# Second convolved tile back in row 6, the first chunks' gate products on VectorE, key-value products later in the recurrence: a two-layer hybrid decoder on one core

## The chip, the cores and the metric

The kernel runs on one core of a Trainium2 chip. Its engines are TensorE (PE in the profile; PEld is its weight load), VectorE (DVE), ScalarE (ACT), GpSimd (POOL) and SyncE (SP), which here only issues DMA transfers. Each engine works through its own queue of instructions in order. The metric is the device time of one execution in microseconds, as the median of several runs. A profile of one execution gives the span from its first to its last instruction.

## What is computed

A decoder of two layers on 1024 tokens of width 1024. Layer 0 mixes tokens with a gated linear recurrence of 8 heads, layer 1 with sliding-window attention; each layer ends with a gated FFN with a causal convolution of width 3. Each sub-layer is followed by a layer norm. Cut to what the change touches:

```python
def hgrn2_chunkwise(q, k, v, log_f):
    # S_t = diag(f_t) S_{t-1} + k_t v_t^T ; o_t = S_t^T q_t, chunk by chunk
    def step(state, inp):
        q_, k_, v_, b_ = inp
        o_inter = jnp.einsum('bhtk,bhkv->bhtv', q_ * jnp.exp(b_), state)
        ...
        o = o_inter + jnp.einsum('bhts,bhsv->bhtv', scores, v_)
        k_dec = k_ * jnp.exp(b_last[:, :, None, :] - b_)
        state = jnp.exp(b_last)[..., None] * state + jnp.einsum('bhsk,bhsv->bhkv', k_dec, v_)
        return state, o

def conv_ffn(h, w_in, conv_w, conv_b, w_out):
    u = h @ w_in
    u = lax.conv_general_dilated(u, conv_w[:, None, :], window_strides=(1,), padding=[(CONV_WIDTH - 1, 0)], ...) + conv_b
    a, b = jnp.split(u, 2, axis=-1)
    return (jax.nn.silu(a) * b) @ w_out
```

The FFN is 2816 wide (w_in is 1024 x 5632), all in float32.

## The kernel before

Every large product is made from a high and a low part of each operand: ScalarE casts a tile to its high part (L249 for weights), VectorE subtracts to get the low part (L197), and TensorE adds three matmuls, high x high, high x low, low x high (`mm3`, L222 to L224). Most products are also cut by a Strassen-like scheme: seven products of half-sized blocks in the place of eight, which need sums of blocks of the weights and of the moving operand, and combinations of the results.

**The order of the work.** In the recurrence the order on all engines is the program's own. A small planner (`Order`) counts TensorE's time in `od.t` while the program is written out. Each piece of a head's work is a generator; a `yield 2.6` says that the next piece is to be emitted once 2.6 us more of TensorE's work have been emitted. In the FFNs only TensorE's order is that of the program; the queues of the other engines, SP's with its DMA issues among them, are ordered by the framework's scheduler from priorities (the program's order) and readiness.

**The recurrence** (`recur`). While the input projections of the next head run in 14 products (`product`, with `evacuate` taking results off the accumulators), the chain of the current head is threaded between them. At its end TensorE turns the decayed keys (8 transposes), ScalarE copies them to `kd` (L1189), the generator pauses at L1190, and TensorE multiplies keys with values (`psax<-VG,kd`, L228 through `mm32`). VectorE then carries the state through the chunks (L1203, L1205), and after another pause TensorE makes the outputs (L1214 to L1217). The chains of the heads follow one another. `VG` holds values and gates of a head and is written by the evacuations of later projections (L1385, L1389).

**The FFN's up-projection** (`Up`). The 2816 columns of each half are made in 22 chunks (`fc`) of 128 for the SiLU half and 128 for the gate half; each chunk has seven products in the order 1, 2, 6, 7, 4, 5, 3 (chunks 0 and 1 are interleaved). A product is 12 matmuls.

- Weights: `weight_load` brings a chunk's two raw pairs of blocks to `rx` buffers (L471), and casts the first. `weight_sums` makes the sums of blocks on VectorE (L480 to L483) and splits them. The raw buffers take turns: `rx[0]`, `rx[1]`, `rx[2]`, and from chunk 2 on also row 7 of `Y`, so that the second pair of chunks 3, 5, 7 and so on goes to row 7, and their first to `rx[2]`.
- Results: `collect` combines the seven results in `Y` rows 0 to 3 (L506 to L520). After product 4 the SiLU half is complete, after product 3 the gate half; each is then convolved: ScalarE writes bias plus the last tap (L526), VectorE adds two shifted taps (L528). The SiLU half is convolved in row 4 or 5 of `Y` (by turns) and passed through SiLU (L531). The gate half is convolved in row 6, in chunk 1 in row 7. Their product (L533) goes back to row 4 or 5, on GpSimd in chunks 0 and 1, on VectorE in the others, and is stored to DRAM (`gd`, L534).
- After chunks 2, 6, 10 and 14 GpSimd's queue adds up blocks of the down-projection's weights by DMA (`bsd`, L549, L551).

Before the up-projection, row 7 of `Y` holds the eighth token block, which is normed, stored and turned (L433 to L445).

Of the kernel before, what the change touches and what calls it, by code (L numbers as in the profile page):

```python
# [14 lines left out]
ALU = mybir.AluOpType  # L15
# [7 lines left out]
NH = 8  # L23
# [111 lines left out]
def trunk(ctx: ExitStack, tc: tile.TileContext, a: dict, out: bass.AP):  # L135
    nc = tc.nc
# [19 lines left out]
    Y = Rows(cp)  # L156
# [239 lines left out]
    tt = nc.vector.tensor_tensor  # L396
# [6 lines left out]
    class Up:  # L403
# [98 lines left out]
        def collect(self, p, fc, ps):  # L502
            l, C = self.l, Y[:, 2 * (fc % 2):2 * (fc % 2) + 2, :]
            C11, C21, C12, C22 = C[:, 0, :512], C[:, 0, 512:], C[:, 1, :512], C[:, 1, 512:]
            if p == 1:
                nc.scalar.copy(C11, ps)  # L506
                nc.scalar.copy(C12, ps)
            elif p == 2:
                tt(C11, C11, ps, op=add)
            elif p == 6:  # L510
                tt(C12, C12, ps, op=add)
            elif p == 7:
                tt(C22, C12, ps, op=add)
            elif p == 4:
                tt(C21, C22, ps, op=add)  # L515
            elif p == 5:
                both = C[:, 1, :].rearrange("p (h n) -> p h n", h=2)
                tt(both, both, ps.unsqueeze(1).to_broadcast([P, 2, 512]), op=add)
            elif p == 3:
                tt(C12, C12, ps, op=add)  # L520
            if p in (4, 3):
                part = 0 if p == 4 else 1
                ci = fc + part * NF
                u, ca = C[:, part, :], Y[:, 4 + fc % 2, :]
                c = Y[:, 7 if fc == 1 else 6, :] if part else ca
                nc.scalar.activation(c, u, AF.Identity, bias=cwt[:, l, 3, ci:ci + 1], scale=cwt[:, l, 2, ci:ci + 1])  # L526
                for sh in (1, 2):
                    nc.vector.scalar_tensor_tensor(c[:, sh:], u[:, :S - sh], cwt[:, l, 2 - sh, ci:ci + 1],  # L528
                                                   c[:, sh:], op0=ALU.mult, op1=ALU.add)
                if part == 0:  # L530
                    nc.scalar.activation(c, c, AF.Silu)  # L531
                else:
                    (nc.gpsimd if fc < 2 else nc.vector).tensor_tensor(ca, ca, c, op=ALU.mult)  # L533
                    nc.sync.dma_start(gd[:, fc, :], ca)  # L534
                    if fc in (2, 6, 10, 14):
                        k = 3 * (fc // 4)
                        self.sums_of_weights(k, min(k + 3, NF // 2), ca[:1, :16])
# [186 lines left out]
    with tc.tile_pool(name="t", bufs=1, reuse_waits="tile") as raws, hgrn_pool as hp:  # L724
# [320 lines left out]
        def recur(h, qs, fg, kp):  # L1045
# [141 lines left out]
            put()  # L1187
            kd = hp.tile([P, S], F32, name="kd")
            nc.scalar.copy(kd, ps)  # L1189
            yield 2.6 if h < NH - 2 else 2.0  # L1190
            while values_in[0] < h:
                yield 0.2
            V = VG[h][:, 0, :].rearrange("p (c d) -> p c d", c=NB)
# [281 lines left out]
        with tc.manual_schedule(engines={EN.PE, EN.SP, EN.Activation, EN.DVE, EN.Pool}):  # L1475
# [11 lines left out]
            def all_heads():  # L1487
                h = -1
                while h < NH - 1:
                    while not ready:  # L1490
                        yield 0.2
                    h, args = ready.pop(0)
                    yield from recur(h, *args)
# [8 lines left out]
            for n, (m, p) in enumerate(line):  # L1502
# [4 lines left out]
                h, g = pairs[m]  # L1507
# [413 lines left out]
```

## Time and profile before

| | us |
|---|---|
| median of 3 runs | 2131.01 |
| lowest, highest run | 2129.49, 2133.35 |
| the profiled execution | 2129.32 |
| its span, first to last instruction | 2127.5 |

The mean granted clock of TensorE over the span is 0.993 of full speed. Layer 0's recurrence takes about the first 460 us, its output projection and FFN run to about 1230, attention to about 1420, and layer 1's FFN to the end.

How to read the rows: a row of a timeline has the start and the duration in us, the engine, the line of the kernel, the operation, the tile written `<-` the tiles read, shapes and a count; in brackets stands how long the engine was idle before it and what ended that. A row of merged instructions gives the time from the first one's start to the last one's end. A row `A <- B: total, times, longest` of the list of waits says how long A waited for B. The name `Y` is that of the whole group of rows, so that rows 4, 6 and 7 have the same name in the profile.

### The profile page before, as it was taken

What the parts mean: (1) busy time and instruction counts of PE and PEld (TensorE: products, weight loads), DVE (VectorE), ACT (ScalarE), POOL (GpSimd) and SP (SyncE); (2) the same over time, 40 slices, a digit from 0 to 9 for tenths busy, and PEclk for the clock granted to TensorE, in tenths of its full rate; (3) what the DMA queues carried; (4) which work ended last, traced back from release to release, by engine and by line L of the source; (5) the groups of instructions that cost most, each with busy time, mean ns of one, the idle gap of its engine ahead of it and who ended that gap; (6) DMA issues with size and microseconds to landing.
All of it is one profiled execution on the core that took longest, in us unless ns stands there. A gap on an engine that the chain in (4) does not pass through costs nothing.

```text
span 2127.5 us, 31578 instructions
## 1 busy us (share of the span) xinstructions
PE 2091.0 (98%) x12303; PEld 1742.4 (82%) x12303; DVE 1777.9 (84%) x2420; ACT 970.5 (46%) x1586; POOL 189.1 (9%) x214
## 2 busy tenths in 40 slices
PE   9999999999989999999999999999989999999998
PEld 8778888787878888888888888888868888888886
DVE  6777777768989999987977679979989999878986
ACT  6556555643534444444433367733444444444430
POOL 1000000001010000000001123312100000000002
PEclk9999999999999999999999999999999999999999
DMA  4111111333256775538755511052275776449662
GB/s 153 41 51 51 51 51 51 118 119 117 80 146 161 183 178 150 142 109 303 248 187 164 143 36 46 18 174 89 70 177 149 178 183 152 121 146 323 228 211 97
DMA packets 239824, 286.82 MB, mean 135 GB/s; under 512 B 30217, under 2 KB 160441, under 8 KB 239417
## 3 DMA queue, kind: packets, MB, share of 16 engines
q1 hardware_dynamic: 223360, 238.26, 34.6%
q0 software_dynamic: 15456, 46.16, 10.9%
q8 instruction: 97, 1.59, 0.3%
q14 instruction: 55, 0.44, 0.1%
q10 hardware_dynamic: 856, 0.37, 0.1%
HBM read 241.72 MB, written 89.15 MB: 156 GB/s over the span
## 4 chain that ended last, share of the span: by engine, by line
PE 68%; DVE 3%; DMA 0%; issue 0%; ACT 0%; POOL 0%; SPq 0%; DVEq 0%; POOLq 0%; ACTq 0%
PE psmm L224 13%; PE psmm L222 12%; PE psmm L223 12%; PE psax L222 9%; PE psax L224 9%; PE psax L223 9%; PE psmm L228 1%; PE psax L1695 1%; PE psmm L232 1%; DVE Y L528 1%; DVE HL L197 0%; PE psax L232 0%; DMA rx<-in_ffn_w_in_dram 0%; DMA Y<-in_ffn_w_in_dram 0%; DVE TX L197 0%
## 5 line engine op out<-in xcount | busy, mean ns | idle before, releaser
L222 PE MATMUL psmm<-T,HL 128*128 128x512 f32 x816 | 322.4, 395 | 0.5 <-DVE VG L758 0.4
L223 PE MATMUL psmm<-T,HL 128*128 128x512 f32 x816 | 318.3, 390 | 0.9 <-DVE T L197 0.9
L224 PE MATMUL psmm<-T,HL 128*128 128x512 f32 x816 | 318.5, 390 | 0.2 <-DVE HL L197 0.2
L528 DVE SCALAR_TENSOR_TENSOR Y<-Y,cwt,Y 128x1023 f32<-128x1023 f32 (+1 forms) x176 | 226.7, 1290 | 47.3 <-ACT Y L526 45.8
L249 ACT CAST HL<-rx 128x1024 fp32r<-128x1024 f32 (+1 forms) x151 | 151.0, 1006 | 175.4 <-DMA rx<-in_ffn_w_in_dram 44.7
L197 DVE TENSOR_TENSOR HL<-rx,HL 128x1024 fp32r<-128x1024 f32 (+1 forms) x151 | 177.1, 1179 | 25.2 <-ACT HL L249 25.0
L224 PEld LDWEIGHTS psmm<-T,HL 128*128 128x128 f32 x816 | 153.3, 188 | 32.7 <-DVE HL L197 0.6
L222 PEld LDWEIGHTS psmm<-T,HL 128*128 128x128 f32 x816 | 153.4, 188 | 31.9 <-DVE VG L758 0.7
L223 PEld LDWEIGHTS psmm<-T,HL 128*128 128x128 f32 x816 | 153.5, 188 | 31.6 <-DVE T L197 1.3
L222 PE MATMUL psax<-T,HL 128*128 128x512 f32 x392 | 153.4, 391 | 0.0
L224 PE MATMUL psax<-T,HL 128*128 128x512 f32 x392 | 152.7, 390 | 0.0
L223 PE MATMUL psax<-T,HL 128*128 128x512 f32 x392 | 152.7, 390 | 0.0
L526 ACT ACTIVATE Y<-Y,cwt 128x1024 f32<-128x1024 f32 x88 | 108.8, 1237 | 91.4 <-DVE Y L515 91.4
L197 DVE TENSOR_TENSOR HL<-raw,HL 128x512 fp32r<-128x512 f32 (+1 forms) x121 | 92.3, 790 | 38.0 <-ACT HL L1303 27.0
L271 POOL TENSOR_TENSOR rs<-rs,nhalf 128x1 f32<-128x1 f32 x32 | 45.0, 1406 | 740.9 <-DVE rs L270 740.9
L249 ACT CAST HT<-rx 128x1024 fp32r<-128x1024 f32 (+1 forms) x37 | 35.5, 959 | 125.2 <-DVE rx L482 48.4
L222 PE MATMUL psmm<-HL 128*128 128x512 f32 x220 | 86.5, 393 | 0.0
L223 PEld LDWEIGHTS psax<-T,HL 128*128 128x128 f32 x392 | 74.0, 189 | 15.3
L222 PEld LDWEIGHTS psax<-T,HL 128*128 128x128 f32 x392 | 73.9, 189 | 15.1
L224 PEld LDWEIGHTS psax<-T,HL 128*128 128x128 f32 x392 | 73.6, 188 | 15.3
L224 PE MATMUL psmm<-HL 128*128 128x512 f32 x220 | 85.8, 390 | 0.0
L223 PE MATMUL psmm<-HL 128*128 128x512 f32 x220 | 85.8, 390 | 0.0
(404 smaller groups left out, 5209.9 us busy)
## 6 DMA issues: line engine op xcount, KB each, us to landing
rx<-in_ffn_w_in_dram SPq DMA_DIRECT2D x136, 256.0 KB
rx<-gd SPq DMA_DIRECT2D x118, 256.0 KB
bsd<-in_ffn_w_out_dram POOLq DMA_DIRECT2D x36, 768.0 KB, 8.2
gd<-Y SPq DMA_DIRECT2D x44, 512.0 KB
raw<-in_hgrn_w_in_dram SPq DMA_DIRECT2D x30, 512.0 KB
rx<-in_ffn_w_out_dram SPq DMA_DIRECT2D x54, 256.0 KB
R<-bsd SPq DMA_DIRECT2D x44, 256.0 KB
Y<-in_ffn_w_in_dram SPq DMA_DIRECT2D x40, 256.0 KB
```

The source lines that it names most:

```text
L197: make = lambda e: e.tensor_tensor(lo, src, hi.bitcast(F32), op=ALU.subtract)
L222: nc.tensor.matmul(ps, st(0), mv(0), start=start, stop=False, skip_group_check=onto)
L223: nc.tensor.matmul(ps, st(0), mv(1), start=False, stop=False, skip_group_check=onto)
L224: nc.tensor.matmul(ps, st(1), mv(0), start=False, stop=stop, skip_group_check=onto)
L228: nc.tensor.matmul(ps, lhsT, rhs, start=start, stop=stop, **kw)
L232: nc.tensor.transpose(ps, src, ident)
L249: nc.scalar.copy(hi, src)
L271: nc.gpsimd.tensor_tensor(rs, rs, nhalf, op=ALU.pow)
L526: nc.scalar.activation(c, u, AF.Identity, bias=cwt[:, l, 3, ci:ci + 1], scale=cwt[:, l, 2, ci:ci + 1])
L528: nc.vector.scalar_tensor_tensor(c[:, sh:], u[:, :S - sh], cwt[:, l, 2 - sh, ci:ci + 1], c[:, sh:], op0=ALU.mult, op1=ALU.add)
L1695: nc.tensor.matmul(self.pv[:, e, jj, lo:], self.q[bp // 2][es, e, qs], Kl[es, pp, ks] if low else Kh[:, pp, e, ks], start=not low and jj = ...
```

## The change

It does three things:

1. The convolved gate half (`c`) lies in row 6 of `Y` in every chunk. Before, chunk 1 used row 7.
2. The gate products of chunks 0 and 1 are made by VectorE, as those of the other chunks already were, two in each layer.
3. The pause between the copy of `kd` and the products of keys with values is 5.0 in heads 0 and 1 and 3.4 in heads 2 to 5; it was 2.6 in heads 0 to 5. Heads 6 and 7 keep 2.0.

```diff
@@ -522,7 +522,7 @@
                 u, ca = C[:, part, :], Y[:, 4 + fc % 2, :]
-                c = Y[:, 7 if fc == 1 else 6, :] if part else ca
+                c = Y[:, 6, :] if part else ca
                 nc.scalar.activation(c, u, AF.Identity, bias=cwt[:, l, 3, ci:ci + 1], scale=cwt[:, l, 2, ci:ci + 1])
@@ -530,7 +530,7 @@
                 else:
-                    (nc.gpsimd if fc < 2 else nc.vector).tensor_tensor(ca, ca, c, op=ALU.mult)
+                    tt(ca, ca, c, op=ALU.mult)
                     nc.sync.dma_start(gd[:, fc, :], ca)
@@ -1187,7 +1187,7 @@
             nc.scalar.copy(kd, ps)
-            yield 2.6 if h < NH - 2 else 2.0
+            yield 5.0 if h < 2 else 3.4 if h < NH - 2 else 2.0
             while values_in[0] < h:
```

`tt` is `nc.vector.tensor_tensor`; `NH` is 8.

## The prediction

> **What bounds the kernel now.** I read the page's busy shares first, then the list of what TensorE waited for, then windows of 40 us, and last the timelines around the waits. The page:
>
> ```profile
> span 2127.5 us, 31578 instructions
> ...
> PE 2091.0 (98%) x12303; PEld 1742.4 (82%) x12303; DVE 1777.9 (84%) x2420; ACT 970.5 (46%) x1586; POOL 189.1 (9%) x214
> ```
>
> TensorE (PE) is idle for 36.5 of 2127.5 us. No matmul is added or removed by the change, so it can win only what TensorE loses: idle time, and matmuls run at a lower clock. Who makes it wait (total, times, longest):
>
> ```profile
> PE psmm L222 <- ACT HL L249: 10.1, 2, 5.3
> PE psax L228 <- ACT kd L1189: 6.0, 3, 2.8
> PE psmm L224 <- DVE HL L197: 2.5, 3, 1.8
> PE psmm L222 <- ACT VG L1385: 0.6, 1, 0.6
> PE psmm L222 <- ACT VG L1389: 0.6, 1, 0.6
> ```
>
> The first and third rows lie in the up-projections of the two FFNs, the second in the recurrence: the two places that the change touches. The windows price the first place (columns: window, length, then busy us and instructions of PE, PEld, DVE, ACT and POOL, granted clock, DMA):
>
> ```profile
> 600.00:640.00 40.00, 34.66 (x140) 27.68 (x139) 32.27 (x39) 17.15 (x20) 3.86 (x5) 0.91 0.71 175
> 640.00:680.00 40.00, 40.00 (x178) 33.15 (x177) 38.37 (x46) 16.66 (x19) 2.43 (x3) 1.00 0.67 169
> 1520.00:1560.00 40.00, 32.91 (x132) 26.31 (x131) 35.71 (x39) 17.46 (x20) 7.80 (x4) 0.87 0.34 108
> ```
>
> An undisturbed 40 us hold 178 matmuls, 0.225 us each. The window of layer 0 holds 140, so 38 x 0.225 = 8.5 us are lost there; that of layer 1 holds 132, so 46 x 0.225 = 10.3 us. Together 18.9 us, more than the idle time alone, since after each wait the clock stands below 1.00. The wait itself in layer 0, and what stands behind it, each engine's row in turn:
>
> ```profile
> 602.68 0.39 PE L224 MATMUL psmm<-T,HL 128*128 128x512 f32 x1
> 607.83 0.80 PE L222 MATMUL psmm<-TX,HL 128*128 128x512 f32 x1 [4.76 <-ACT HL L249]
> ```
>
> ```profile
> 606.74 1.04 ACT L249 CAST HL<-Y 128x1024 fp32r<-128x1024 f32 x1 [1.33 <-DVE Y L482]
> ```
>
> ```profile
> 601.21 0.68 DVE L480 TENSOR_TENSOR rx<-Y,rx 128x512 f32<-128x512 f32 x1
> ```
>
> ```profile
> 560.17 14.97 SPq L471 DMA_DIRECT2D rx<-in_ffn_w_in_dram  x6
> 589.29 6.99 SPq L534 DMA_DIRECT2D gd<-Y  x2
> 596.45 1.18 SPq L471 DMA_DIRECT2D Y<-in_ffn_w_in_dram  x2
> ```
>
> ```profile
> 593.50 2.41 POOL L533 TENSOR_TENSOR Y<-Y 128x1024 f32<-128x1024 f32 x1 [4.24 <-DVE Y L528]
> ```
>
> From the bottom up: GpSimd's (POOL's) product for chunk 1 reads row 7 of Y until 595.91. Only then can SP issue the load of half of chunk 3's weights into that same row (596.45). VectorE (DVE) sums them from 601.21, ScalarE (ACT) casts the sum at 606.74, and the product that needs it, due at 602.68 + 0.23 = 602.91, starts at 607.83, as the cast ends. Layer 1 repeats it, and there the landing shows too: 1535.28 to 1538.73 is 3.45 us from issue to use.
>
> ```profile
> 1531.53 3.22 POOL L533 TENSOR_TENSOR Y<-Y 128x1024 f32<-128x1024 f32 x1 [1.25 <-DVE Y L528]
> ```
>
> ```profile
> 1535.28 1.19 SPq L471 DMA_DIRECT2D Y<-in_ffn_w_in_dram  x2
> ```
>
> ```profile
> 1538.73 0.69 DVE L480 TENSOR_TENSOR rx<-Y,rx 128x512 f32<-128x512 f32 x1 [0.18 <-DMA Y<-in_ffn_w_in_dram]
> ```
>
> ```profile
> 1548.81 0.80 PE L222 MATMUL psmm<-TX,HL 128*128 128x512 f32 x1 [5.32 <-ACT HL L249]
> ```
>
> **Row 6 for both chunks.** With chunk 1's second tile in row 6, nothing writes row 7 between the turning of the eighth token block and chunk 3's load. SP issued the loads of chunks 2, 3 (its other half) and 4 from 560.17 to 575.14; row 7's two loads can now join them. If they go at the end of that stretch they land by 575.14 + 3.45 = 578.6. From first use to matmul the longer of the two chains took 1548.81 - 1538.73 = 10.1 us, so the weights stand at 588.7, 14 us before 602.91. Both stalls go whole: 18.9 us.
>
> The price is a new wait. ScalarE's L526 of chunk 1 writes row 6 and must wait until chunk 0's product has read it; behind it on ScalarE's queue stand weight casts and the next chunk's convolution. The cover is ScalarE's own idle time:
>
> ```profile
> 594.01 1.25 ACT L526 ACTIVATE Y<-Y,cwt 128x1024 f32<-128x1024 f32 x1 [5.50 <-DVE Y L515]
> ```
>
> The wait is about one product on VectorE, 1.2 us, inside 5.50 us of idleness: cost nothing. Without that cover 1.2 us per layer.
>
> **Products on VectorE.** Four products move. By engine (ns min/median/max), then two rows of VectorE while GpSimd's ran:
>
> ```profile
> L533 DVE TENSOR_TENSOR Y<-Y x40: 1217/1225/1227, 606.6 to 1920.2; 128x1024 f32<-128x1024 f32 x40
> ...
> L533 POOL TENSOR_TENSOR Y<-Y x4: 2409/2817/3227, 586.8 to 1531.5; 128x1024 f32<-128x1024 f32 x4
> ```
>
> ```profile
> 593.85 2.60 DVE L480 TENSOR_TENSOR rx<-rx,rx 128x512 f32<-128x512 f32 x1
> ```
>
> ```profile
> 1533.02 2.28 DVE L197 TENSOR_TENSOR HL<-rx,HL 128x512 fp32r<-128x512 f32 x1
> ```
>
> VectorE gains 4 x 1.225 = 4.9 us of work. But under GpSimd's products two 128x512 operations took 2.60 and 2.28 us instead of the 0.69 of the row at 1538.73, 3.5 us longer in all. So VectorE's load changes by +1.4 us if these two are the whole of it, by +4.9 us if GpSimd is not their cause; I take +1.4, 0.7 per layer. It matters because VectorE is full there:
>
> ```profile
> 581.75:612.50 30.75, 25.41 (x104) 20.13 (x103) 30.71 (x32) 13.99 (x16) 6.15 (x4) 0.92 0.25 83
> ```
>
> 30.71 of 30.75 us. What hides the added 0.7 us is that part of this run was for chunk 4, not due for another 19 us (7 products of 12 matmuls), while chunk 3's sums waited for row 7; with row 7 early chunk 3 can go first. I cost it at nothing and keep the other case as a rival.
>
> **The later key-value products.** The plan counts a step of a projection (three matmuls) as 3 x 512 / 2365 + 0.031 = 0.68 us. A pause of 2.6 lets 4 steps pass, 5.0 lets 8 pass, 3.4 lets 5 pass: four steps, 2.72 us, come ahead of the products of heads 0 and 1, one step ahead of those of heads 2 to 5. Heads 0, 1 and 4 wait today, all for the copy of kd:
>
> ```profile
> 92.83 0.39 PE L224 MATMUL psmm<-Y,HL 128*128 128x512 f32 x1
> 95.77 3.35 PE L228 MATMUL psax<-VG,kd 128*128 128x128 f32 x14 [2.55 <-ACT kd L1189]
> ```
>
> ```profile
> 94.71 1.01 ACT L1189 COPY kd<-psax 128x1024 f32<-128x1024 f32 x1
> ```
>
> ```profile
> 145.11 0.39 PE L224 MATMUL psmm<-T,HL 128*128 128x512 f32 x1
> 148.27 1.83 PE L228 MATMUL psax<-VG,kd 128*128 128x128 f32 x14 [2.77 <-ACT kd L1189]
> ```
>
> ```profile
> 147.21 1.01 ACT L1189 COPY kd<-psax 128x1024 f32<-128x1024 f32 x1
> ```
>
> ```profile
> 297.75 1.83 PE L228 MATMUL psax<-VG,kd 128*128 128x128 f32 x14 [0.68 <-ACT kd L1189]
> ```
>
> Head 0: TensorE's next slot is 93.06; four steps later it is 95.78, and kd is ready at 95.72. All 2.71 us go, and the fourteen products, 3.35 us here against 1.83 at head 1, regain 1.5. Head 1: the slot moves to 148.06, kd is ready at 148.22; 0.2 of 2.93 us stay, 2.7 go. Head 4: one step covers the 0.68. Together 4.2 + 2.7 + 0.7 = 7.6 us. On the copy's own engine nothing moves ahead of it. Moved later are VectorE's state updates, the norms on ScalarE and the head's store on SP; every chain runs serially, so heads 1 and 2 start later against the projections. What is late next is an evacuation that such a chain holds up: the two 0.6 us waits for VG. I double them: -1.2 us of gain. Below, that could be nothing; above, the whole 7.6 us.
>
> The clock decides 1.5 us of this:
>
> ```profile
> 95.60:99.00 3.40, 3.23 (x15) 3.23 (x16) 0.00 (x0) 2.67 (x5) 0.00 (x0) 0.50 0.90 251
> 145.30:151.30 6.00, 3.23 (x21) 2.80 (x21) 4.24 (x9) 4.92 (x10) 0.00 (x0) 1.00 0.06 13
> ```
>
> A stop of 2.55 us halved the clock, one of 2.77 us did not. The Trainium skill ("TensorE: Matmul & The Clock Gate", "Why this matters for your kernels") advises to keep TensorE's idle gaps under about 3 us, as a window of idleness halves the clock; by it neither stop would have cost clock, and the gain here would be 6.1 instead of 7.6 us. The trace disagrees at head 0, and I go by the trace.
>
> **Sum.** The profiled execution took 2129.3 us, its span plus 1.8. 2129.3 - 18.9 - 7.6 + 1.2 = 2104.0. It ran 1.7 us under the median of the runs, 2131.0; against that median I expect 2105.7, so 2106.
>
> **Rivals**, each on the median's scale.
> - VectorE becomes the bound (0.10). Against it: the chunk-4 work ahead of its due time; for it: 30.71 of 30.75. If its order stays, half of each stall stays: 18.9 / 2 = 9.4 us less gain, 2115.
> - The recurrence gives nothing (0.14): chains late by 2.72 us per head stop evacuations elsewhere. 2106 + 6.4 = 2112.
> - The change doesn't do what it says (0.09): SP's order keeps chunk 3's load behind the two stores of gd, as in the row at 589.29, and the stalls stay. 2106 + 18.9 = 2125.
> - Slower (0.04): chunk 0's product is queued on VectorE behind its whole full run, to 612.5; L526 then holds ScalarE's casts. Chunk 3's cast follows and TensorE restarts 1.1 us later (606.74 to 607.83), at 613.6: 10.7 us idle, plus 5.2 us of clock (0.13 of 40 us, as in layer 1's window), 15.9 per layer. 2106 + 31.8 = 2138. It decides once it costs over 25 / 2 = 12.6 us a layer, that is idle of 7.4 us, the product ending past 609. Against it: the product stands before chunk 2's work in the program. The Trainium skill ("TensorE: Matmul & The Clock Gate", "Architectural detail") calls the queues of ScalarE and VectorE strictly first-in first-out, by which such a wait would hold all that follows; no run here shows that case yet.
>
> **Chances.** My forecast has 0.60, the rivals 0.37, 0.03 lie about no change. About 0.2%, 4.3 us, is what a measurement of this kernel can tell from none: faster is under 2126.7, slower over 2135.3. Faster holds the forecast and the first three rivals, less a little for a mixture of them: 0.88; same 0.07; slower 0.05. The range starts where the 1.2 us are not lost, the 1.7 us between profile and median are not there, and a run falls 1.5 us to the good side, as the lowest (2129.5) did: 2106 - 4.4, rounded down to 2101. It ends past VectorE's case, 2115, with the 2.3 us by which the highest run (2133.4) lies over the median, rounded up to 2118. The third and fourth rivals lie outside.
>
> **What would show it.** In the new profile SP's loads of row 7 stand before the stores of gd, near 575; no idle at chunk 3's third product, 178 matmuls in both windows; no POOL row at L533 and no VectorE operation of 128x512 over 1 us there; waits for kd under 0.5 us in total. I am wrong if TensorE stops at another product of chunks 2 to 4, if waits for evacuations in the recurrence exceed 3 us, or if the loads still follow the stores.

## The result, and the profile after

The changed kernel takes 2112.14 us, the median of 5 runs (2110.97 to 2113.66), against 2131.01 us before: a ratio of 0.991, 95% interval 0.9896 to 0.9924. The forecast was 2106, with a range of 2101 to 2118. The profiled execution took 2113.66 us, the longest of the five, where the one before (2129.32 us) lies under all five times of its kernel (from 2129.49); so the profiles differ by less than the medians. The gain of the FFNs came as forecast; that of the recurrence, 6.4 us in the sum, did not come at all. The page of the changed kernel:

```profile
span 2111.9 us, 31565 instructions
...
PE 2087.5 (99%) x12303; PEld 1739.4 (82%) x12303; DVE 1774.9 (84%) x2424; ACT 972.2 (46%) x1586; POOL 177.5 (8%) x210
```

The span fell by 15.6 us. TensorE is now idle for 24.4 us of it, 12.1 less than before; the other 3.5 are busy time, from matmuls that no longer run at a lower clock. The list of what TensorE waited for, at the places of the change:

```profile
PE psax L228 <- ACT kd L1189: 4.9, 2, 2.6
...
PE psax L232 <- ACT VG L1391: 0.6, 2, 0.3
...
PE psmm L222 <- DVE VG L1397: 0.4, 1, 0.4
```

The rows for L249 and L197 of the two up-projections are gone. The row for `kd` is still there: 6.0 us in three waits became 4.9 us in two. The windows over the two old stalls:

```profile
600.00:640.00 40.00, 40.00 (x179) 33.12 (x178) 36.19 (x42) 16.15 (x18) 3.33 (x4) 1.00 0.68 171
640.00:680.00 40.00, 40.00 (x178) 33.17 (x177) 39.86 (x47) 18.34 (x21) 2.94 (x4) 1.00 0.75 195
1520.00:1560.00 40.00, 40.00 (x178) 33.14 (x177) 40.00 (x45) 18.91 (x21) 2.38 (x3) 1.00 0.44 131
```

178 or 179 matmuls where there were 140 and 132, at full clock. Layer 0's chunk 3 in the timelines of SP, VectorE, ScalarE and TensorE:

```profile
558.97 0.92 SPq L471 DMA_DIRECT2D Y<-in_ffn_w_in_dram  x2
562.32 21.26 SPq L471 DMA_DIRECT2D rx<-in_ffn_w_in_dram  x8
592.10 7.40 SPq L534 DMA_DIRECT2D gd<-Y  x2
```

```profile
572.45 0.69 DVE L480 TENSOR_TENSOR rx<-Y,rx 128x512 f32<-128x512 f32 x1
...
590.85 1.22 DVE L533 TENSOR_TENSOR Y<-Y 128x1024 f32<-128x1024 f32 x1
```

```profile
592.10 1.25 ACT L526 ACTIVATE Y<-Y,cwt 128x1024 f32<-128x1024 f32 x1 [1.10 <-DVE Y L533]
```

```profile
606.19 0.39 PE L222 MATMUL psmm<-TX,HL 128*128 128x512 f32 x1
```

Row 7's load now stands ahead of the other loads and 33 us ahead of the stores of `gd`; the first sum that reads it comes 28.8 us earlier than before; the new wait of L526 is there, 1.10 us, inside idle time. The third product starts at 606.19 without a wait.

**Where the recurrence's gain went.** One matmul of the output projection can serve as a marker for the end of the recurrence, in the timeline of TensorE before and after:

```profile
468.60 0.49 PE L222 MATMUL psmm<-HL,T 128*128 128x512 f32 x1 [0.31 <-ACT T L249]
```

```profile
471.64 0.51 PE L222 MATMUL psmm<-HL,T 128*128 128x512 f32 x1 [0.31 <-ACT T L249]
```

Up to here the changed kernel is 3.0 us later, so from here on it is 15.6 + 3.0 = 18.6 us shorter; the two FFN stalls had been put at 18.9. The waits of heads 0, 1 and 4 for `kd` have gone as forecast, but heads 2 and 3, which did not wait before, now do. Head 2 before, in the timeline of all engines (the last row is cut by the view's end):

```profile
188.78 1.09 PE L232 MATMUL psax<-ident,kp 128*128 128x128 f32 x8
...
189.96 1.01 ACT L1189 COPY kd<-psax 128x1024 f32<-128x1024 f32 x1 [0.30 <-PE psax L232]
...
190.87 0.63 ACT L1015 ACTIVATE fg<-fg 128x512 f32<-128x512 f32 x1
...
192.46 0.72 PE L228 MATMUL psax<-VG,kd 128*128 128x128 f32 x5
```

and after:

```profile
192.39 0.63 ACT L1015 ACTIVATE fg<-fg 128x512 f32<-128x512 f32 x1
...
194.07 1.09 PE L232 MATMUL psax<-ident,kp 128*128 128x128 f32 x8
...
197.24 0.60 ACT L1015 ACTIVATE fg<-psmm 128x512 f32<-128x512 f32 x1
...
200.10 1.01 ACT L1189 COPY kd<-psax 128x1024 f32<-128x1024 f32 x1
...
201.17 1.18 PE L228 MATMUL psax<-VG,kd 128*128 128x128 f32 x6 [2.58 <-ACT kd L1189]
```

Before, ScalarE was idle when the transposes (L232) came and copied at once; the next head's forget gate (L1015) followed the copy. After, the same work stands ahead of it: ScalarE is busy without a gap from 191.87, works through casts and both halves of the forget gate, and copies 4.9 us after the transposes' end. The longer pause at head 2 covers one step of a projection (0.68 us), not this. Head 3 shows the same with 2.36 us. The clock paid too:

```profile
201.70:205.10 3.40, 3.40 (x15) 3.15 (x14) 0.93 (x3) 0.42 (x1) 0.00 (x0) 0.50 0.22 65
252.90:256.30 3.40, 3.40 (x13) 2.92 (x12) 2.54 (x7) 2.93 (x5) 0.00 (x0) 0.50 0.31 77
```

Two such windows stand in the recurrence, where before there was one. Of the 3.0 us: -1.1 for `kd`, +1.0 for waits for VG (0.6 us of L1391 and 0.4 of L1397 are new), +1.7 for one more halved window of 3.41 us; 1.4 us I cannot assign to rows. The marker also moves by itself: with the old pauses it stands at 468.60 in the kernel before, but at 471.49, 467.00 and 469.47 in the executions of e1, e3 and e4 below, which met three, no and two halved windows up to there where the kernel before met one; with the new pauses it stands at 471.64 here, and at 470.41 and 469.25 in e2 and e11. So the 3.0 us alone are no measure of what the pauses cost.

### The profile page after: what moved, and what is told of

Its sections match the earlier page's. It is cut to its first block, busy times and chain, and to the rows that moved or that the text cites. A ratio compares the mean times of both kernels' runs of the same rounds, so it can differ in the third digit from the quotient of the medians.

```text
span 2111.9 us, 31565 instructions
## 1 busy us (share of the span) xinstructions
PE 2087.5 (99%) x12303; PEld 1739.4 (82%) x12303; DVE 1774.9 (84%) x2424; ACT 972.2 (46%) x1586; POOL 177.5 (8%) x210
## 3 DMA queue, kind: packets, MB, share of 16 engines
q8 instruction: 97, 1.59, 0.3%
## 4 chain that ended last, share of the span: by engine, by line
PE 92%; DVE 4%; ACT 2%; issue 1%; DMA 0%; SPq 0%; DVEq 0%; ACTq 0%
PE psmm L222 18%; PE psmm L223 18%; PE psmm L224 18%; PE psax L222 10%; PE psax L224 10%; PE psax L223 10%; PE psax L228 3%; PE psmm L232 2%; PE psmm L228 1%; PE psax L1695 1%; PE psax L232 1%; PE psmm L1542 1%; DVE HL L197 1%; DVE T L197 0%; DVE qp L1118 0%
## 5 line engine op out<-in xcount | busy, mean ns | idle before, releaser
L249 ACT CAST HL<-rx 128x1024 fp32r<-128x1024 f32 (+1 forms) x151 | 151.5, 1007 | 176.5 <-DMA rx<-in_ffn_w_in_dram 38.2
L197 DVE TENSOR_TENSOR HL<-rx,HL 128x1024 fp32r<-128x1024 f32 (+1 forms) x151 | 174.9, 1163 | 18.5 <-ACT HL L249 18.3
L526 ACT ACTIVATE Y<-Y,cwt 128x1024 f32<-128x1024 f32 x88 | 108.8, 1237 | 87.6 <-DVE Y L515 85.1
L197 DVE TENSOR_TENSOR HL<-raw,HL 128x512 fp32r<-128x512 f32 (+1 forms) x121 | 92.3, 789 | 39.8 <-ACT HL L1303 29.2
L249 ACT CAST HT<-rx 128x1024 fp32r<-128x1024 f32 (+1 forms) x37 | 35.5, 959 | 131.0 <-DVE rx L482 62.1
```

Of the source, the lines that this page charges most:

```text
L197: make = lambda e: e.tensor_tensor(lo, src, hi.bitcast(F32), op=ALU.subtract)
L249: nc.scalar.copy(hi, src)
```

## The experiments

Theory: the FFN edits give the whole gain, the pauses nothing, since heads 0 and 1, paused longer, shift the later chains so that the copies of heads 2 and 3 come up on ScalarE behind the next head's gates. Rivals: each pause acts on its own head; or TensorE's order, not ScalarE's queue, makes the waits. All medians, with the ratio to the kernel before on the same chip:

| run | us, lowest to highest | ratio, 95% interval |
|---|---|---|
| e1_ffn_only | 2110.81, 2110.13 to 2111.82 | 0.9919, 0.9905 to 0.9932 |
| e2_pauses_only | 2129.08, 2126.63 to 2131.94 | 1.0006, 0.9997 to 1.0015 |
| e3_row6_gpsimd | 2115.15, 2111.79 to 2118.01 | 0.9943, 0.9928 to 0.9958 |
| e4_row7_vector | 2122.36, 2120.46 to 2124.20 | 0.9972, 0.9962 to 0.9982 |
| e5_first_heads | 2110.34, 2109.07 to 2111.04 | 0.9917, 0.9902 to 0.9933 |
| e6_later_heads | 2108.43, 2106.59 to 2109.51 | 0.9908, 0.9892 to 0.9924 |
| e7_kd_vector | 2109.65, 2109.10 to 2110.40 | 0.9915, 0.9900 to 0.9930 |
| e8_kd_vector_pauses | 2103.99, 2103.63 to 2106.04 | 0.9891, 0.9872 to 0.9909 |
| e9_last_head_scalar | 2100.01, 2098.76 to 2100.71 | 0.9867, 0.9854 to 0.9881 |
| e10_planner_only | 2107.41, 2104.47 to 2108.26 | 0.9900, 0.9887 to 0.9914 |
| e11_changed_again | 2111.89, 2109.89 to 2112.48 | 0.9922, 0.9909 to 0.9936 |
| e12_engine_only | 2104.95, 2104.34 to 2106.60 | 0.9888, 0.9871 to 0.9904 |

e1 to e4 ran beside a median of 2128.71 us before, e5 to e8 beside 2127.51, e9 to e11 beside 2128.05, e12 beside 2129.49.

**The parts alone.** e1 is the changed kernel with the old pauses:

```diff
-            yield 5.0 if h < 2 else 3.4 if h < NH - 2 else 2.0
+            yield 2.6 if h < NH - 2 else 2.0
```

> The FFN's two edits alone (row 6 in every chunk, gate products on VectorE); the pauses of the recurrence as before. Theory: the FFN's edits take away both stalls of chunk 3 whole (18.7 us by the spans: the profile after ends 15.6 us earlier although its recurrence ends 3.05 us later), and the later key-value products cost about 3 us. Then this kernel takes about 2131.0 - 18.7 = 2112.3 or less than the changed kernel by 3 us, 2109 to 2112, with kd waits at heads 0, 1 and 4 as before. Rival: the pauses gained the 6.4 us that were forecast and the FFN only the other 12.5; then about 2118.5.

e2 is the kernel before with the new pauses alone (the same line, the other way round).

> The pauses of the changed kernel alone, the FFN as before. Theory: the waits for kd move from heads 0, 1 and 4 to heads 2 and 3, each with a halved clock behind it; the recurrence ends about 3 us later: 2133 to 2135, stalls at chunk 3 in both layers as before. Rival: the pauses gain by themselves and only lose beside the FFN's edits: about 2124.6.

e1 took 2110.81 us, 17.9 below the kernel before beside it: it has the whole gain. e2 took 2129.08, within 0.2% of it: the pauses bring nothing that can be measured. Its waits show both sides at once, the old FFN stalls and the new waits for `kd`:

```profile
PE psmm L222 <- ACT HL L249: 9.5, 2, 5.1
PE psax L228 <- ACT kd L1189: 4.9, 2, 2.6
```

So the waits of heads 2 and 3 come with the pauses and need no change in the FFN. My 3 us of loss for e2 was too much; the measurement allows up to 0.15% (3.2 us), its middle is 1.3 us. The markers say about the same, as an estimate: less 1.7 us for each halved window of 3.41 us, they stand at 466.1 to 467.0 with the old pauses and at 467.5 to 468.7 with the new ones.

**Row 6 and VectorE apart.** e3 keeps row 6 for both chunks and makes the products on GpSimd again; e4 keeps row 7 for chunk 1 and makes them on VectorE. Both have the old pauses; the edits are shown against the changed kernel.

```diff
-                    tt(ca, ca, c, op=ALU.mult)
+                    (nc.gpsimd if fc < 2 else nc.vector).tensor_tensor(ca, ca, c, op=ALU.mult)
```

> Row 6 in every chunk, but chunks 0 and 1 keep their gate products on GpSimd; pauses as before. Theory that row 7 alone makes the stalls: no stall at chunk 3, within 1 us of the kernel with the FFN's edits alone, 2109 to 2113, although two or more VectorE operations are stretched to 2 us and more under GpSimd's products. Rival, that GpSimd's products make them (slow, and holding up VectorE): stalls of some us remain, over 2118.

```diff
-                c = Y[:, 6, :] if part else ca
+                c = Y[:, 7 if fc == 1 else 6, :] if part else ca
```

> Row 7 kept for chunk 1, gate products on VectorE; pauses as before. Theory that row 7 alone makes the stalls: SP's load of row 7 still follows the stores of gd, both stalls stay within 2 us of their size, 2128 to 2134. Rival, that GpSimd's products make them: most of 18.9 us is gained, under 2120.

Both expectations missed. e3's median lies 4.3 us over e1's (their intervals just touch, 0.9928 against 0.9932), with one stop left, in layer 0. Its profiled execution is its fastest and as long as e1's, but no halved window fell in its recurrence: from the marker (467.00, in e1 471.49) to the end it takes 4.6 us longer. The timeline there:

```profile
583.78 3.77 POOL L533 TENSOR_TENSOR Y<-Y 128x1024 f32<-128x1024 f32 x1 [42.94 <-DVE Y L528]
...
587.59 1.24 ACT L526 ACTIVATE Y<-Y,cwt 128x1024 f32<-128x1024 f32 x1 [3.35 <-POOL Y L533]
...
588.87 1.28 DVE L528 SCALAR_TENSOR_TENSOR Y<-Y,cwt,Y 128x1023 f32<-128x1023 f32 x1 [2.97 <-ACT Y L526]
...
592.11 2.41 POOL L533 TENSOR_TENSOR Y<-Y 128x1024 f32<-128x1024 f32 x1 [4.55 <-DVE Y L528]
...
592.46 2.61 DVE L482 TENSOR_TENSOR Y<-Y,rx 128x512 f32<-128x512 f32 x1
...
601.45 1.21 DVE L197 TENSOR_TENSOR HL<-Y,HL 128x1024 fp32r<-128x1024 f32 x1
...
602.71 0.73 PE L224 MATMUL psmm<-TX,HL 128*128 128x512 f32 x1 [2.76 <-DVE HL L197]
```

With one row for two chunks, GpSimd's slow product of chunk 0 holds L526 (3.35 us), VectorE waits for L526 (2.97 us), and under the second product VectorE's sum L482 takes 2.61 us. VectorE, which has no room there, makes the low part of chunk 3's weights (601.45) only after TensorE needs it (at 599.80, where the next matmul's turn had come), and TensorE stops. So the product on VectorE is not a side matter of the change: it is what makes row 6 cheap. In e4, where I expected the stalls whole, the waits for L249 are halved (10.1 us before, 5.0 here) and a third of the gain is there. The timeline:

```profile
591.38 1.22 DVE L533 TENSOR_TENSOR Y<-Y 128x1024 f32<-128x1024 f32 x1
...
593.07 1.25 SPq L471 DMA_DIRECT2D Y<-in_ffn_w_in_dram  x2
...
606.12 0.74 PE L222 MATMUL psmm<-TX,HL 128*128 128x512 f32 x1 [3.54 <-ACT HL L249]
```

The load still waits for the product that reads row 7, but VectorE has that done by 592.60 where GpSimd had it by 595.91, and the load goes at 593.07, not 596.45. In the medians, row 6 alone gains 13.6 us, VectorE alone 6.3, both 17.9. That the two gains overlap isn't shown: their sum, 19.9, lies within the intervals.

**Which pauses.** e5 and e6 are the changed kernel with only one of the two pauses new.

```diff
-            yield 5.0 if h < 2 else 3.4 if h < NH - 2 else 2.0
+            yield 5.0 if h < 2 else 2.6 if h < NH - 2 else 2.0
```

> The changed kernel's FFN, with the long pause of 5.0 at heads 0 and 1 only; heads 2 to 5 keep the old 2.6. It tells which of the two pauses brings the new waits for the kd copies of heads 2 and 3. Theory (the long pauses of the first two heads make every later step of those chains late, so that the copies of heads 2 and 3 come up on ScalarE behind the next projections' gates): heads 0, 1 and 4 without a kd wait, or head 4 with its old 0.7 us; heads 2 and 3 again with 2 to 3 us each; the end of the recurrence within 2 us of the changed kernel's 471.3 us; time 2110 to 2114 us, the same as the changed kernel. Rival (each head's own pause sets its own wait): heads 2 and 3 free of waits, end of the recurrence near 466 us, time near 2107 us.

```diff
-            yield 5.0 if h < 2 else 3.4 if h < NH - 2 else 2.0
+            yield 2.6 if h < 2 else 3.4 if h < NH - 2 else 2.0
```

> The changed kernel's FFN, with the old pause of 2.6 at heads 0 and 1 and the new 3.4 at heads 2 to 5. Theory (lateness comes from the first two heads): kd waits at heads 0 and 1 as in the kernel before, 2.5 to 3 us each, none or little at heads 2, 3 and 4; end of the recurrence 468 to 471 us, time 2109 to 2112 us. Rival (each head's own pause sets its own wait): heads 2 and 3 wait 2 to 3 us as well, four waits together, end of the recurrence near 475 us, time near 2116 us.

In e5 heads 2 and 3 wait 3.24 and 2.83 us though their own pauses are the old ones:

```profile
201.68 1.62 PE L228 MATMUL psax<-VG,kd 128*128 128x128 f32 x7 [3.24 <-ACT kd L1189]
```

```profile
252.18 2.05 PE L228 MATMUL psax<-VG,kd 128*128 128x128 f32 x12 [2.83 <-ACT kd L1189]
```

(Head 6 waits too, 0.96 us.) In e6 they have the longer pauses and do not wait; only heads 0 and 1 do, 2.55 and 2.96 us. So the new waits come from the lateness that heads 0 and 1 hand on, and the rival, each pause its own wait, falls. In time the two cannot be told from the changed kernel or from e1: the intervals overlap. e6's 2108.43 us lies a little under its theory's 2109.

**The engine of the copy.** e7 and e8 move the copy to VectorE and tell the planner of its 1.2 us (`od.vec`, a note of how long VectorE is taken, from which the planner puts off later pieces), e7 with the old pauses, e8 with the new ones.

```diff
-            nc.scalar.copy(kd, ps)
+            nc.vector.tensor_copy(kd, ps)
+            od.vec(1.2)
```

> The changed kernel's FFN, old pauses of 2.6, and the copy of the keys' products out of PSUM on VectorE where it was on ScalarE. Theory (the copy is late because of what stands ahead of it on ScalarE): no wait for kd at heads 0, 1 and 4 above 0.6 us, end of the recurrence 464 to 468 us, time 2105 to 2109 us. Rival (the copy follows the transposes too closely for any engine, or VectorE has as much ahead of it): waits of 1 to 3 us stay at these heads, now for VectorE, time 2110 to 2113 us.

> The changed kernel with nothing but that copy moved from ScalarE to VectorE; the new pauses stay. Theory (ScalarE's gates ahead of the copies of heads 2 and 3 make these two wait): the waits at heads 2 and 3 go, no kd wait above 0.6 us is left, end of the recurrence 465 to 468 us, time 2105 to 2109 us. Rival (it is the later order of TensorE's own work, or VectorE is as busy there): waits of 2 us or more stay at heads 2 and 3, time 2110 to 2114 us.

e8 did as the theory said: no wait for `kd` is left, 2103.99 us. e7 did not: head 1 still stops, now for VectorE:

```profile
143.99 0.69 DVE L197 TENSOR_TENSOR HL<-raw,HL 128x512 fp32r<-128x512 f32 x1 [3.12 <-ACT HL L1304]
144.59 1.22 DVE L1189 COPY kd<-psax 128x1024 f32<-128x1024 f32 x1
...
145.96 1.38 PE L228 MATMUL psax<-VG,kd 128*128 128x128 f32 x9 [2.04 <-DVE kd L1189]
```

VectorE stood idle for 3.12 us, but at the head of its queue was a split that waits for ScalarE's cast, and the copy behind it. Here the other engine helped little, since its queue hung on the first. With the long pause (e8) head 1 has the time, and with the copy on VectorE the change's pauses pay: 5.7 us between e7 and e8 on one chip, with no overlap of the runs.

In e8, however, the planner's note also moves TensorE's pieces. e10 is its control: the note alone, the copy left on ScalarE. e11 is the changed kernel once more, on the same chip. e9 is e8 with head 7's copy on ScalarE, without the note there, aimed at a stop that e8 has in the output projection.

```diff
             nc.scalar.copy(kd, ps)
+            od.vec(1.2)
```

> A control: the changed kernel with the copy left on ScalarE, and only the planner told of 1.2 us of VectorE work at that place, as it is where VectorE does the copy. Theory (the gain of 8 us came from the copy's engine): the waits at heads 2 and 3 stay at 2 to 3 us each, time 2111 to 2114 us, as the changed kernel. Rival (the gain came from the planner's new due times, which move TensorE's pieces): the waits go, time 2104 to 2107 us.

> The changed kernel as it is, beside the other two on one chip. All theories: 2111 to 2114 us, with its waits at heads 2 and 3 of 2.6 and 2.4 us; only the halved-clock windows of 3.41 us behind them may be none, one or two.

```diff
-            nc.scalar.copy(kd, ps)
+            if h < NH - 1:
+                nc.vector.tensor_copy(kd, ps)
+                od.vec(1.2)
+            else:
+                nc.scalar.copy(kd, ps)
```

> The version with the copy of the keys' products on VectorE and the new pauses, except that head 7's copy goes back to ScalarE. In that version a stop of 2.65 us stands in the output projection at 439.61, for the second of two splits of 128x1024 on VectorE, and head 7's copy (1.23 us) is one of the pieces ahead of them. Theory (VectorE's row of work is the wait): the stop shrinks by about 1.2 us to 1.4 us, no kd wait comes at head 7, and the time is 2102 to 2104 us. Rival (the splits are late because TensorE delivers late, not by VectorE's row): the stop stays at 2.4 us or more, time 2103.5 to 2105 us.

e10 went against the theory: with the copy on ScalarE it still took 4.5 us less than e11 on the same chip, and no run of the one reaches those of the other. Its head 2:

```profile
186.93 1.09 PE L232 MATMUL psax<-ident,kp 128*128 128x128 f32 x8
...
190.78 1.01 ACT L1189 COPY kd<-psax 128x1024 f32<-128x1024 f32 x1
...
191.84 1.38 PE L228 MATMUL psax<-VG,kd 128*128 128x128 f32 x10 [0.39 <-ACT kd L1189]
```

The chain comes 7 us earlier there, the copy 2.8 us behind the transposes in the place of 4.9, and the pause covers all but 0.39 us; 0.94 us are left at head 6. Why the note makes the chain earlier I have not followed. So e8 doesn't show that the engine decides; e12 asks that alone, with every piece in the changed kernel's order (TensorE's list of instructions is the same, row for row).

```diff
-            nc.scalar.copy(kd, ps)
+            nc.vector.tensor_copy(kd, ps)
```

> The changed kernel with the copy of the keys' products on VectorE and the planner not told of it, so that every piece stands in the changed kernel's order. With the planner told, the copy left on ScalarE had lost its waits too; this run has the engine alone. First theory (the copy's engine decides): the waits at heads 2 and 3 go, no kd wait above 0.6 us, time 2105 to 2108 us. Second theory (the order decides: in this order the splits that follow ScalarE's casts stand ahead of the copy on VectorE too; by the changed kernel's rows they end at 198.02 at head 2 and 251.53 at head 3, and TensorE is there at 198.59 and 249.42): with 1.22 us for the copy a wait of 0.6 to 1.5 us stays at head 2 and one of 2.4 to 3.4 us at head 3, time 2109 to 2112 us.

```profile
195.84 1.22 DVE L1189 COPY kd<-psax 128x1024 f32<-128x1024 f32 x1
...
198.50 1.72 PE L228 MATMUL psax<-VG,kd 128*128 128x128 f32 x14
```

```profile
246.60 1.80 PE L228 MATMUL psax<-VG,kd 128*128 128x128 f32 x14 [1.59 <-DVE kd L1189]
```

Head 2's wait goes whole: the copy stands ahead of the splits that I had put before it. Head 3 keeps 1.59 of 2.36 us: there the copy stands on VectorE behind a split (L197 at 244.63) that waited for ScalarE's cast, as at head 1 of e7. So neither theory has both heads right. The time, 2104.95 us, lies a hair below the first theory's 2105. It ran on another chip than e11, but all its runs (up to 2106.60 us) are shorter than all ten of the changed kernel (from 2109.89), and its ratio's interval ends under that of e11 (0.9904 against 0.9909), though not under that of the changed kernel's first measurement (from 0.9896). With TensorE's order the same, ScalarE's queue ahead of the copy is thereby shown as the cause of head 2's new wait, and of head 3's at least in the part that went. There are two cures: take the copy off that queue (e12), or move the chain (e10). Whether both together (e8) beat e10 is not settled; the intervals overlap.

e9 aimed at this stop of e8, and e10 has it too:

```profile
442.37 1.22 DVE L197 TENSOR_TENSOR T<-qs,T 128x1024 fp32r<-128x1024 f32 x1
443.50 1.22 DVE L197 TENSOR_TENSOR T<-kp,T 128x1024 fp32r<-128x1024 f32 x1
...
443.64 0.73 PE L1543 MATMUL psmm<-HL,T 128*128 128x512 f32 x2 [2.65 <-DVE T L197]
```

With head 7's copy on ScalarE in e10, VectorE's copy can't be its cause, so e9's theory falls; its rival, that the stop stays, did not come either. It is the order again: with the note at head 7 the splits of qs and kp stand behind the state's updates on VectorE (they begin at 442.37 and 443.50 here, after 439.86 to 442.46 for the updates), without it before them (432.20 and 433.34 in e9, the updates from 437.45), and e9's stop is gone entirely. e9 takes 2100.01 us: faster than the kernel before by a ratio of 0.9867 (0.9854 to 0.9881), and than the changed kernel on the same chip by 11.9 us, with no overlap of the runs. It has the lowest median of the versions; on its chip it lies 7.4 us under e10, but its interval overlaps those of e8 and e12, which ran on another.

## Why the prediction was right or wrong

- **Row 6 frees row 7 for an early load: right,** in its mechanism (SP's rows at 558.97 and 592.10) and, with the products on VectorE, in size (18.9 us; 18.6 in the profiles, 17.9 in e1's medians). But the 18.9 us were put down to the row alone, and e3 has the row alone: 13.6. The load went ahead of the others, not behind them at 575.
- **The new wait of L526 costs nothing: right,** 1.10 us inside idle time; the price had been 1.2. e3 shows what it costs with a slower product.
- **Products on VectorE cost nothing: right.** VectorE is busy for 25.55 of the 26 us from 580 on, and TensorE does not stop. VectorE's load, put at +1.4 us, fell from 1777.9 to 1774.9 us. That the products on VectorE gain by themselves (e4) I had not seen.
- **The later products: wrong.** The waits of heads 0, 1 and 4 went as worked out. The step that failed: "On the copy's own engine nothing moves ahead of it." I held each head's copy at its old time and moved only TensorE's products. But I had written myself that heads 1 and 2 start later against the projections, and did not carry that to ScalarE, whose gates belong to the projections and don't move. e2, e5, e6 and e12 show it: the 6.0 us of waits and one halved window (1.7 us) went, and 4.9 us of waits with two such windows (3.4 us) came at heads 2 and 3. My own sign, waits for `kd` under 0.5 us in total, failed by that. The waits for evacuations, 1.0 us more, are near the 1.2 that I had deducted, but the two that I had doubled (L1385, L1389) did not change; the new ones are at L1391 and L1397.
- **The clock at head 0: wrong as a sure gain.** I counted 1.5 us for a halved window; the last section shows that it is there in some executions only.
- The rival "the recurrence gives nothing" gave the time, 2112; its mechanism, evacuations, was only a small part of it. So the forecast of 2106 missed by 6 us, nearly the whole term of the recurrence.

## What to carry to other kernels

Making one piece of a serial chain later makes every following piece later against the work that is not in the chain: list, for each engine that the chain uses, what the shift puts ahead of it, not only at the edited step but one turn on. Before a wait is covered by a pause, ask what the awaited engine does before the awaited instruction; taking it off the busy queue gained about 7 us (e12), and moving the chain to where the queue was shorter 4.5 (e10), where the pause gained nothing. And an edit that frees a buffer can need its neighbour: row 6 alone and the faster product alone each left stalls that only both removed.

## What the runs showed of the hardware

**The clock's price of a stop depends on its moment.** Head 0's stop of 2.53 to 2.55 us occurs in five kernels with the same code there: the clock halved behind it in the kernel before and in e1, and not in e3, e4 and e6. The changed kernel itself shows it in two executions: head 2's stop of 2.58 us was followed by the halved window at 201.70 above, but in e11 by full clock. e3's window after head 0's stop, then e11's row and window of head 2:

```profile
96.00:99.40 3.40, 3.40 (x23) 3.02 (x22) 1.79 (x6) 2.64 (x5) 0.00 (x0) 1.00 1.04 298
```

```profile
200.48 1.83 PE L228 MATMUL psax<-VG,kd 128*128 128x128 f32 x14 [2.58 <-ACT kd L1189]
```

```profile
200.50:203.90 3.40, 3.40 (x22) 3.10 (x23) 1.41 (x5) 1.09 (x3) 0.00 (x0) 1.00 0.39 118
```

In e7 the clock was halved behind a stop of 2.04 us (the row at 145.96 above):

```profile
146.70:150.10 3.40, 3.40 (x15) 3.01 (x14) 1.82 (x6) 0.88 (x2) 0.00 (x0) 0.53 0.02 5
```

The halved stretches last 3.41 us or a multiple, and begin on a grid: in the changed kernel at 201.70 and 252.90, 51.20 us apart, 15 times 3.413, though the stops before them end 50.61 us apart (201.17 and 251.78). In e1 two stretches begin at 96.35 and 147.55, again 51.20 us apart, the first 0.60 us after its stop's end and the second, of two windows, 0.82 us before it. The Trainium skill ("TensorE: Matmul & The Clock Gate", Part 1 on the clock gate) has a window of 3413 ns that runs freely; the trace agrees. As an estimate from these rows, a stop of 2 to 3 us costs no clock, one window (1.7 us) or two by where it falls, which would make part of the 2 us by which runs of one kernel differ. No run here shifted a stop to test it.

**VectorE under GpSimd.** e3's L482 begins at 592.46 and ends at 595.07, 0.55 us after GpSimd's product has ended (592.11 + 2.41 = 594.52); undisturbed (at 572.45 in the changed kernel) such an operation takes 0.69. The Trainium skill ("SBUF — State Buffer", the section on the two separate sides) says that the port pair which the two share is locked for a whole instruction, and the other waits; it says so of a VectorE instruction with both inputs in SBUF, the on-chip memory, against a GpSimd instruction that reads there, as here: the trace agrees. In the other order, GpSimd's first product in e3, begun at 583.78 while VectorE worked on two splits from 583.48 to 585.30, took 3.77 us, where its second took 2.41.
